# Loading the first projection's weights behind the first token tile, and transposing later token tiles ahead of their own projection, in a five-layer transformer kernel

## Chip, cores and metric

The kernel runs on one core of a Trainium2 chip. The metric is the device time of one launch in microseconds; the time before is the median of three runs. The profile is of a fourth execution, which the hardware profiler recorded.

## What is computed

Five blocks in fp32 on 512 tokens of width 1024: layers of the kinds MLA, SWA, FOX and again MLA, and then a second block of mixers, a gated feed-forward part and a last gate. Only the first steps of the first MLA layer matter here:

```python
h = x @ w_in
cq, ckv, k_rope, gate = h[..., :c1], h[..., c1:c2], h[..., c2:c3], h[..., c3:]
q = (_rmsnorm(cq, q_norm) @ w_q_up).reshape(B, S, MLA_HEADS, MLA_NOPE_DIM + MLA_ROPE_DIM)
kv = (_rmsnorm(ckv, kv_norm) @ w_kv_up).reshape(B, S, MLA_HEADS, MLA_NOPE_DIM + MLA_V_DIM)
```

`cq` has 384 columns, `ckv` 256, `k_rope` 32.

## The kernel before

Tokens are handled in four tiles of 128 (T = 4), the width of 1024 in eight blocks of 128. Each fp32 operand is held as a high part and a low part (`hi`, `lo`), and each product is three matmuls (`mm3`, lines 155 to 159): hi by hi, lo by hi, hi by lo.

**Start.** `__init__` loads the identity. `run` calls `load_x`, which loads the four token tiles (512 KB each) and transposes each on PE with the identity (`to_T`, line 248: two groups of four 128x128 transposes into a PSUM tile `ps_t`, of which there are two; ACT copies the high part, line 184, DVE subtracts for the low part, line 185). Then `mla` loads the tables `cos` and `sin`, and calls `latent` for `ckv` and `k_rope` (288 columns) and again for `cq` (384 columns).

**One latent projection.** `latent` calls `v_proj`. That first asks for eight weight units (`pair_units` for `ckv`): `w` (line 131) loads a unit into a `wr` buffer (there are six), ACT casts it to the high part (L138), POOL or DVE subtracts for the low part (L139). Then, for each token tile, 24 matmuls (8 blocks by 3) fill a PSUM tile `ps_acc` (three buffers), and `evac` normalises that tile: ACT squares and sums (L568), DVE scales the sum (L569), POOL takes the power (L570), DVE multiplies (L571), ACT copies the rope columns (L573), and PE transposes the result (L576 two or three times, L578 once for the rope columns), after which ACT and DVE split it again.

**After the latents** come 24 matmuls of the first gate (512 columns), and then the products on `cq`, the first of which is PE's matmul `ps_acc<-cq,wh` on L157.

**Order.** A scheduler in the build places the instructions of all engines by its own cost estimates, so the order on an engine is not the order of the code. On the chip, each engine takes its instructions in the order placed. SP issues all DMAs; the program gives them eight semaphores in turn (DMAHW0 to DMAHW7), and a DMA waits until the one eight before it has landed, so at most eight are on the way.

Of the kernel before, what the change touches and what calls it, by code (L numbers as in the profile page):

```python
# [15 lines left out]
P, S, D, T = 128, 512, 1024, 4  # L16
# [53 lines left out]

NORM = ("2222", "1122", "0111", "1111")

FOFF = [0, 128, 384, 768]


class Act:


    def __init__(s, hi, lo, n):
        s.hi, s.lo, s.n = hi, lo, n  # L80
# [8 lines left out]
class Kern:  # L89
    def __init__(s, ctx, tc, I, C):  # L90
        s.tc, s.nc, s.I, s.C = tc, tc.nc, I, C
        s.ctx = ctx
        s.sb = ctx.enter_context(tc.tile_pool(name="sb", bufs=1))
        s.dram = ctx.enter_context(tc.tile_pool(name="dram", bufs=1, space=bass.MemoryType.DRAM))
        s.phase_pool, s.phase_tags = None, {}
        s.ps = ctx.enter_context(tc.tile_pool(name="ps", bufs=1, space=PSUM))
        nc = s.nc
        s.ident = s.const("c_ident")
        s.small = s.sb.tile([P, 32], F32, name="small")
        nc.vector.memset(s.small[:, 0:4], -0.5)  # L100
        nc.vector.memset(s.small[:, 4:5], 1e-6)
        nc.vector.memset(s.small[:, 5:6], 1.0)
        s.x = []
        s.rel = None
        s.step = 48

# [159 lines left out]
    def pair_units(s, W, n, c0, cn, dve=False):  # L266

        us = []
        if "hid" in s.phase_tags:
            for k in range(0, n, 2):  # L270
                u = s.t("hid", [P, 4, S], R)
                us += [s.w(W, k + e, 1, c0, cn, u[:, 2 * e:2 * e + 1], u[:, 2 * e + 1:2 * e + 2], dve and e) for e in range(2)]
            return us
        for k in range(n):
            nq = s.phase_tags["qk"]
            if k >= nq + s.phase_tags.get("v", 0):
                us.append(s.w(W, k, 1, c0, cn, "pth", "ptl", dve and k % 2))
            else:
                u = s.t("qk" if k < nq else "v", [P, 2, S], R)
                us.append(s.w(W, k, 1, c0, cn, u[:, :1, :cn], u[:, 1:, :cn], dve and k % 2))  # L280
        return us

    def out_proj(s, W, o, evac, banks=None, oi=5, split_last=False):
# [196 lines left out]
    def mla(s, j, li, xT, g_next):  # L480
        nc, I = s.nc, s.I
        if s.x:
            s.spill_x()
        Win, Wq, Wkv, Wo = I["mla_w_in"][j], I["mla_w_q_up"][j], I["mla_w_kv_up"][j], I["mla_w_out"][j]
        cos = s.t("rope", [P, S], name="cos")
        sin = s.t("rope", [P, S], name="sin")
        nc.sync.dma_start(cos, s.C["c_cos"])
        nc.sync.dma_start(sin, s.C["c_sin"])
        krf = s.t("f", [32, S])
        ckv = s.latent(Win, 384, 288, 256, I["mla_kv_norm"][j], xT, "ckv", krf)  # L490
        cq = s.latent(Win, 0, 384, 384, I["mla_q_norm"][j], xT, "cq")
        kr = s.t("kr", [32, 2, S], R)
        s.rope(krf, cos[:32], sin[:32], kr, 32)
        oT = s.act(8)
        scale = 96.0 ** -0.5
        G = {}

        def queries(g):
            us = [s.w_heads(Wq, k, g * 384, 64, 32) for k in range(3)]
            ps = s.p("acc")  # L500
            for k in range(3):
                h, l = us[k]
                s.mm3(ps, h[:, 256:], l[:, 256:], cq.h(k), cq.l(k), k == 0, k == 2)
            qr = s.t("qr", [P, 2, S], R)
            s.rope(ps, cos, sin, qr, P)
            return us, qr

        def values(g):
            us = [s.w_heads(Wkv, k, g * 512, 64, 64) for k in range(2)]
            vt = [s.t("x", [P, T, 2, 2, 64], R, name="v") for _ in range(2)]  # L510
            for t in range(T):
                ps = s.p("acc")
                c = slice(t * P, (t + 1) * P)
                for k in range(2):
                    h, l = us[k]
                    s.mm3(ps[:, :256], ckv.h(k)[:, c], ckv.l(k)[:, c], h[:, 256:], l[:, 256:], k == 0, k == 1)
                s.v_split(ps[:, :256], [v[:, t] for v in vt])
            return us, vt

        def prep(p):  # L520
            g, pr = divmod(p, 2)
            if ("q", g) not in G:
                G["q", g] = queries(g)
            q_us, qr = G["q", g]
            c = slice(pr * P, (pr + 1) * P)
            ps = s.p("acc")
            for k in range(3):
                h, l = q_us[k]
                s.mm3(ps, h[:, c], l[:, c], cq.h(k), cq.l(k), k == 0, k == 2)
            rr = lambda e: slice(64 * pr + 32 * e, 64 * pr + 32 * e + 32)  # L530
            qt = s.split_heads(ps, lambda e: qr[rr(e)])
            if ("v", g) not in G:
                G["v", g] = values(g)
            kv_us, vt = G["v", g]
            ps = s.p("acc")
            for k in range(2):
                h, l = kv_us[k]
                s.mm3(ps, h[:, c], l[:, c], ckv.h(k), ckv.l(k), k == 0, k == 1)
            kt = s.split_heads(ps, lambda e: kr)
            if pr and g < 3:  # L540
                G["q", g + 1] = queries(g + 1)
            return qt, kt, vt[pr]

        def head(d, p, e):
            qt, kt, v = d
            (qh, ql), (kh, kl) = s.parts(qt[e]), s.parts(kt[e])

            def s_mm(out, i, k0):
                c, kk = slice(i * P, (i + 1) * P), slice(k0 * P, (i + 1) * P)
                return s.mm3(out, qh[:96, c], ql[:96, c], kh[:96, kk], kl[:96, kk], True, True)  # L550

            return s.attend(s_mm, [0] * T, s.causal, scale, s.vsel(v, e))

        s.pairs(range(8), prep, head, Win, 672, xT, oT)
        return s.layer_end(Wo, oT, li, g_next)
# [70 lines left out]
    def v_proj(s, W, c0, n, a, evac, more="p", first=False):  # L626

        kk = 2 if n <= 256 else 1
        if kk == 2:
            us = [s.w(W, k, kk, c0, n) for k in range(0, a.n, kk)]  # L630
        elif more == "p":
            ph, pl = s.t("p", [P, 2, n], R), s.t("p", [P, 2, n], R)
            us = ([s.w(W, k, 1, c0, n, dve=first) for k in range(a.n - 2)]
                  + [s.w(W, a.n - 2 + i, 1, c0, n, ph[:, i:i + 1], pl[:, i:i + 1], first) for i in range(2)])
        else:
            us = s.pair_units(W, a.n, c0, n, first)
        for t in range(T):
            ps = s.p("acc")
            c = slice(t * P, (t + 1) * P)
            for k in range(a.n):  # L640
                h, l = us[k // kk]
                s.mm3(ps[:, :n], a.h(k)[:, c], a.l(k)[:, c], h[:, k % kk], l[:, k % kk], k == 0, k == a.n - 1)
            evac(t, ps)
# [38 lines left out]
    def fox(s, j, li, xT, g_next):  # L682
# [40 lines left out]
        def prep(p):  # L723
# [9 lines left out]
            for e in range(2):  # L733
                cr = s.bcast_row(rows[2 * p + e], "rope")
                b = s.t("qr" if e else "qk", [P, 2, S], name="b").rearrange("p a b -> p (a b)")
                for i in range(3):
                    nc.gpsimd.tensor_add(b[:, FOFF[i]:FOFF[i + 1]], cr[:, :(i + 1) * P], s.causal(i))
                nc.gpsimd.tensor_add(cr[:, 384:], cr[:, 384:], s.causal(0))
                bs.append([b[:, FOFF[i]:FOFF[i + 1]] for i in range(3)] + [cr])
            qt = s.split_q(qps or s.proj(Win, p * P, P, xT))  # L740
# [21 lines left out]
        nc.gpsimd.tensor_sub(lo, a[:n], hi.bitcast(F32))  # L762

    def load_x(s, x, xT):
        for t in range(T):
            xt = s.t("x", [P, D])
            s.nc.sync.dma_start(xt, x[t * P:(t + 1) * P])
            s.to_T(xt, t, xT)
        s.x_src = x
        s.spilled = False  # L770
        s.mask = None
# [365 lines left out]
```

## Time and profile before

| | us |
|---|---|
| runs of before | 1758.92, 1760.01, 1761.11 (median 1760.01) |
| profiled execution, its time | 1762.84 |
| profiled execution, its span | 1761.1 |

The profiled execution's own time is 2.83 us above the median of the runs; its span, first to last instruction, is 1.7 us shorter than that time. Times in the trace count from the span's start. PE was busy for 96% of the span, DVE 55%, ACT 50%, POOL 49%; the mean granted clock of TensorE was 0.979. Idle time of an engine matters only where PE, or the end, waits for it.

### The profile page before, as it was taken

What the parts mean: (1) busy time and instruction counts of PE and PEld (TensorE: products, weight loads), DVE (VectorE), ACT (ScalarE), POOL (GpSimd) and SP (SyncE); (2) the same over time, 40 slices, a digit from 0 to 9 for tenths busy, and PEclk for the clock granted to TensorE, in tenths of its full rate; (3) what the DMA queues carried; (4) which work ended last, traced back from release to release, by engine and by line L of the source; (5) the groups of instructions that cost most, each with busy time, mean ns of one, the idle gap of its engine ahead of it and who ended that gap; (6) DMA issues with size and microseconds to landing.
All of it is one profiled execution on the core that took longest, in us unless ns stands there. A gap on an engine that the chain in (4) does not pass through costs nothing.

```text
span 1761.1 us, 25691 instructions
## 1 busy us (share of the span) xinstructions
PE 1684.8 (96%) x8818; PEld 1435.2 (81%) x8818; DVE 962.0 (55%) x2223; ACT 873.8 (50%) x2054; POOL 854.4 (49%) x775
## 2 busy tenths in 40 slices
PE   8999999999999999999999998999999999999999
PEld 7888878887788888778888877877778888888877
DVE  4587654677654665766587665599544222210053
ACT  4576543666445655633576642755544333332351
POOL 1644534444255665616644523745644444443571
PEclk9999999999999999999999998999999999999999
DMA  5434534322032333314444523332332333332332
GB/s 169 132 98 114 165 104 124 99 70 87 26 97 81 101 88 93 116 51 127 120 110 103 176 61 74 91 81 64 114 90 83 98 96 96 96 100 80 105 99 72
DMA packets 190339, 173.91 MB, mean 99 GB/s; under 512 B 14280, under 2 KB 154952, under 8 KB 190208
## 3 DMA queue, kind: packets, MB, share of 16 engines
q1 hardware_dynamic: 190208, 172.27, 33.9%
q8 instruction: 70, 1.15, 0.3%
q14 instruction: 61, 0.50, 0.1%
HBM read 150.94 MB, written 6.87 MB: 90 GB/s over the span
## 4 chain that ended last, share of the span: by engine, by line
PE 52%; DVE 9%; ACT 2%; issue 2%; POOL 2%; DMA 1%; SPq 0%; ACTq 0%; POOLq 0%; DVEq 0%
PE ps_acc L157 11%; PE ps_acc L158 11%; PE ps_acc L159 11%; PE ps_s L158 4%; PE ps_s L157 4%; PE ps_s L159 4%; PE ps_o L452 2%; PE ps_t L443 2%; DVE p L427 1%; DVE sel L926 1%; ACT p L419 1%; DVE m L925 1%; DVE p L403 1%; PE ps_s L238 1%; DVE ptl L185 1%
## 5 line engine op out<-in xcount | busy, mean ns | idle before, releaser
L139 POOL TENSOR_TENSOR wl<-wr,wh 128x512 fp32r<-128x512 f32 (+2 forms) x362 | 472.7, 1316 | 421.5 <-ACT wh L138 408.7
L138 ACT CAST wh<-wr 128x512 fp32r<-128x512 f32 (+2 forms) x368 | 223.6, 613 | 364.9 <-PE ps_acc L158 125.1
L157 PE MATMUL ps_acc<-act,wh 128*128 128x512 f32 (+1 forms) x880 | 331.5, 377 | 0.9 <-DVE v L620 0.8
L158 PE MATMUL ps_acc<-act,wh 128*128 128x512 f32 (+1 forms) x880 | 330.2, 375 | 0.3 <-DVE act L185 0.2
L159 PE MATMUL ps_acc<-act,wl 128*128 128x512 f32 (+1 forms) x880 | 330.1, 375 | 0.0
L157 PEld LDWEIGHTS ps_acc<-act,wh 128*128 128x128 f32 x880 | 165.6, 188 | 27.9 <-PE ps_acc L159 1.2
L159 PEld LDWEIGHTS ps_acc<-act,wl 128*128 128x128 f32 x880 | 165.3, 188 | 27.5
L158 PEld LDWEIGHTS ps_acc<-act,wh 128*128 128x128 f32 x880 | 165.4, 188 | 27.0 <-DVE act L185 0.7
L419 ACT ACTIVATE p<-p,st 128x256 f32<-128x256 f32 (+3 forms) x288 | 153.5, 537 | 32.8 <-DVE st L410 17.3
L157 PE MATMUL ps_acc<-wh,act 128*128 128x256 f32 (+3 forms) x384 | 134.5, 350 | 7.7 <-ACT act L469 3.1
L185 DVE TENSOR_TENSOR ptl<-ps_t,pth 128x512 fp32r<-128x512 f32 (+1 forms) x200 | 117.6, 597 | 38.5 <-ACT pth L184 37.7
L184 ACT CAST pth<-ps_t 128x512 fp32r<-128x512 f32 (+1 forms) x200 | 100.3, 516 | 72.5 <-PE ps_t L443 63.0
L443 PE MATMUL ps_t<-c_ident,p 128*128 128x128 f32 x672 | 116.9, 283 | 17.3 <-DVE p L427 12.4
L427 DVE TENSOR_SCALAR p<-p,st 128x256 f32<-128x256 f32 (+3 forms) x264 | 132.1, 559 | 1.8
L159 PE MATMUL ps_acc<-wh,act 128*128 128x256 f32 (+3 forms) x384 | 130.7, 341 | 0.1
L158 PE MATMUL ps_acc<-wl,act 128*128 128x256 f32 (+3 forms) x384 | 130.4, 340 | 0.0
L443 PEld LDWEIGHTS ps_t<-c_ident,p 128*128 128x128 f32 x672 | 82.0, 143 | 33.7 <-DVE p L427 13.2
L452 PE MATMUL ps_o<-pth,v 128*128 128x256 f32 (+3 forms) x288 | 90.1, 318 | 6.3 <-DVE og L463 4.4
L452 PE MATMUL ps_o<-ptl,v 128*128 128x256 f32 (+3 forms) x288 | 88.2, 335 | 4.3 <-DVE ptl L185 4.2
L157 PEld LDWEIGHTS ps_acc<-wh,act 128*128 128x128 f32 x384 | 77.8, 203 | 16.0 <-ACT act L469 3.3
L158 PEld LDWEIGHTS ps_acc<-wl,act 128*128 128x128 f32 x384 | 77.7, 202 | 5.1 <-issue 0.5
L159 PEld LDWEIGHTS ps_acc<-wh,act 128*128 128x128 f32 x384 | 77.1, 201 | 5.5 <-DVE act L185 0.3
(371 smaller groups left out, 3801.3 us busy)
## 6 DMA issues: line engine op xcount, KB each, us to landing
wr<-in_w_gate_up_dram SPq DMA_DIRECT2D x88, 256.0 KB, 2.8
wr<-in_fox_w_in_dram SPq DMA_DIRECT2D x60, 256.0 KB, 3.1
wr<-in_w_in_dram SPq DMA_DIRECT2D x48, 256.0 KB, 2.9
wr<-in_w_down_dram SPq DMA_DIRECT2D x44, 256.0 KB, 2.6
wr<-in_swa_w_in_dram SPq DMA_DIRECT2D x40, 256.0 KB, 2.9
wr<-in_mla_w_in_dram SPq DMA_DIRECT2D x32, 256.0 KB, 3.1
qk<-qk SPq DMA_DIRECT2D x32, 256.0 KB, 3.1
wr<-in_mla_w_out_dram SPq DMA_DIRECT2D x32, 256.0 KB, 3.5
```

The costliest lines, as they stand in the source:

```text
L138: nc.scalar.copy(h, raw)
L139: (nc.vector if dve else nc.gpsimd).tensor_sub(l, raw, h.bitcast(F32))
L157: mm(out, lh, rh, start=first, stop=False)
L158: mm(out, lh, rl, start=False, stop=False)
L159: return mm(out, ll, rh, start=False, stop=last)
L184: s.nc.scalar.copy(hi, src)
L185: s.nc.vector.tensor_sub(lo, src, hi.bitcast(F32))
L238: mm(out, q[:, e, c], kd[:, kk], start=True, stop=False)
L419: nc.scalar.activation(a, a, AF.Exp, bias=st[:, 1, i:i + 1], scale=scale, accum_out=st[:, 2, i:i + 1])
L427: nc.vector.tensor_scalar_mul(a, a, st[:, 3, i:i + 1])
L443: nc.tensor.transpose(ps[:, n:n + P], sc[:, c:c + P], s.ident)
L452: nc.tensor.matmul(o[:, j * P:j * P + m], vj, pp[:, c:c + m], start=first, stop=k == 1 and grp[-1] == max(2, grp[-1]) and j == grp[-1], sk ...
```

## The change

`load_x` now issues only the first token tile's load, puts ten identity-by-identity transposes into a `ps_t` tile, and leaves two lists: `late_loads` (loads of tiles 1 to 3) and `late` (the transposes of tiles 0 to 3). `pair_units` issues one of the late loads after each of weight units 6, 7 and 8 (k = 5, 6, 7). `v_proj` runs `late[t]` just ahead of the matmuls of token tile t. `mla` asks for `cos` and `sin` after the first `latent`.

```diff
+WARM = 10
...
-        s.x = []
+        s.x, s.late, s.late_loads = [], [], []
...
                 us.append(s.w(W, k, 1, c0, cn, u[:, :1, :cn], u[:, 1:, :cn], dve and k % 2))
+            if k >= 5 and s.late_loads:
+                s.late_loads.pop(0)()
         return us
...
-        nc.sync.dma_start(cos, s.C["c_cos"])
-        nc.sync.dma_start(sin, s.C["c_sin"])
         krf = s.t("f", [32, S])
         ckv = s.latent(Win, 384, 288, 256, I["mla_kv_norm"][j], xT, "ckv", krf)
+        nc.sync.dma_start(cos, s.C["c_cos"])
+        nc.sync.dma_start(sin, s.C["c_sin"])
...
+        late, s.late = s.late, []
         for t in range(T):
+            if late:
+                late[t]()
             ps = s.p("acc")
...
     def load_x(s, x, xT):
-        for t in range(T):
-            xt = s.t("x", [P, D])
-            s.nc.sync.dma_start(xt, x[t * P:(t + 1) * P])
-            s.to_T(xt, t, xT)
+        nc = s.nc
+        xs = [s.t("x", [P, D]) for _ in range(T)]
+        load = lambda t: nc.sync.dma_start(xs[t], x[t * P:(t + 1) * P])
+        load(0)
+        warm = s.p("t")
+        for k in range(WARM):
+            nc.tensor.transpose(warm[:, k % 4 * P:(k % 4 + 1) * P], s.ident, s.ident)
+        s.late_loads = [lambda t=t: load(t) for t in range(1, T)]
+        s.late = [lambda t=t: s.to_T(xs[t], t, xT) for t in range(T)]
```

Lines of the changed kernel are two to seven higher: line 248 becomes 250, 157 to 159 become 159 to 161, 576 and 578 become 580 and 582, 138 becomes 140, 568 becomes 572.

**PE, around the first normalised tile.** Before, the 24 matmuls of three token tiles (72 in all, mixed) stand ahead of the first transposes of a normalised tile; the last of them and what follows:

```order
L157 MATMUL ps_acc<-pth,act 128x288
L158 MATMUL ps_acc<-ptl,act 128x288
L159 MATMUL ps_acc<-pth,act 128x288
L576 MATMUL ps_t<-c_ident,f 128x128 [waits DVE_49]
L576 MATMUL ps_t<-c_ident,f 128x128
L578 MATMUL ps_t<-c_ident,f 32x128 [waits Activation_49]
L157 MATMUL ps_acc<-qk,act 128x288 [waits PE_49]
```

In the change, the same transposes stand behind the 24 matmuls of token tile 0 alone, and ahead of all work of tile 1:

```order
L160 MATMUL ps_acc<-ptl,act 128x288 [waits DVE_49]
L161 MATMUL ps_acc<-pth,act 128x288
L580 MATMUL ps_t<-c_ident,f 128x128 [waits DVE_49]
L580 MATMUL ps_t<-c_ident,f 128x128
L250 MATMUL ps_t<-c_ident,x 128x128 [waits DMAHW1_49,PE_49]
L250 MATMUL ps_t<-c_ident,x 128x128 x3
L582 MATMUL ps_t<-c_ident,f 32x128 [waits Activation_49]
L159 MATMUL ps_acc<-qk,act 128x288 [waits Activation_49]
L160 MATMUL ps_acc<-qk,act 128x288
L250 MATMUL ps_t<-c_ident,x 128x128 [waits DVE_49]
L250 MATMUL ps_t<-c_ident,x 128x128 x3
L161 MATMUL ps_acc<-qk,act 128x288
```

The waits on PE are, in order: for DVE's multiply of tile 0 (f), for the load of token tile 1 (x), for ACT's high part of tile 1's first four blocks, and for DVE's low part of them. The same piece stands between tiles 1 and 2; between 2 and 3 it differs in that 21 matmuls of `cq` (384 columns) stand between the two matmuls and the second group of transposes.

**SP, the first DMAs.** Before:

```order
L110 DMA c_ident<-in_c_ident_dram 128x128
L767 DMA x<-in_x_dram 128x1024 x4
L487 DMA cos<-in_c_cos_dram 128x512
L488 DMA sin<-in_c_sin_dram 128x512
L256 DMA f<-in_mla_kv_norm_dram 128x256
L135 DMA wr<-in_mla_w_in_dram 128x288 [waits DMAHW0_49]
```

In the change:

```order
L112 DMA c_ident<-in_c_ident_dram 128x128
L775 DMA x<-in_x_dram 128x1024
L258 DMA f<-in_mla_kv_norm_dram 128x256
L137 DMA wr<-in_mla_w_in_dram 128x288 x5
L137 DMA wr<-in_mla_w_in_dram 128x288 [waits DMAHW0_49]
L775 DMA x<-in_x_dram 128x1024 [waits DMAHW1_49]
L775 DMA x<-in_x_dram 128x1024 [waits DMAHW2_49]
L137 DMA wr<-in_mla_w_in_dram 128x288 [waits DMAHW3_49,Pool_49]
L137 DMA wr<-in_mla_w_in_dram 128x288 [waits DMAHW4_49,DVE_49]
L775 DMA x<-in_x_dram 128x1024 [waits DMAHW5_49]
```

Six weight units moved ahead of token tiles 1 and 2; units 7 and 8 stand behind those two tiles, because they wait for a `wr` buffer.

**ACT, between the squares of tile 0 and those of tile 1, in the change:**

```order
L572 ACTIVATE f,st<-ps_acc 128x256 [waits PE_49]
L140 CAST wh<-wr 128x384 [waits DMAHW0_49]
L577 COPY f<-ps_acc 128x32 [waits DVE_49]
L140 CAST wh<-wr 128x384 [waits DMAHW1_49]
L140 CAST wh<-wr 128x384 [waits DMAHW2_49]
L186 CAST act<-ps_t 128x4x128 [waits PE_49]
L583 COPY f<-ps_t 32x128 [waits PE_49]
L186 CAST ckv<-ps_t 128x2x128
L140 CAST wh<-wr 128x384 [waits DMAHW3_49]
L140 CAST wh<-wr 128x384 [waits DMAHW6_49]
L140 CAST wh<-wr 128x384 [waits DMAHW7_49]
L186 CAST act<-ps_t 128x4x128 [waits PE_49]
```

Casts of `cq`'s weights (384 columns) moved between the copies of tile 1: three ahead of its first high part, three more ahead of its second, and another two ahead of its squares.

Past the first layer's `cq` the order is the same on all engines, apart from a few places: around the end of the FOX layer and the start of the second MLA layer, groups of up to five matmuls stand up to 40 places earlier or later on PE, and in the second block's mixers some transposes and copies trade places.

## Rows read from the trace of the kernel before

**Rows 1.** The page, busy time of the engines over the span.

```profile
PE 1684.8 (96%) x8818; PEld 1435.2 (81%) x8818; DVE 962.0 (55%) x2223; ACT 873.8 (50%) x2054; POOL 854.4 (49%) x775
```

**Rows 2.** Waits of PE, 0 to 60 us: total us, times, longest us.

```profile
PE ps_t L248 <- DMA x<-in_x_dram: 4.9, 1, 4.9
PE ps_t L576 <- DVE f L571: 2.1, 2, 2.0
```

**Rows 3.** Timeline of PE, 0 to 60 us: start us, us, what [idle before <-releaser].

```profile
4.87 1.94 PE L248 MATMUL ps_t<-c_ident,x 128*128 128x128 f32 x8 [4.87 <-DMA x<-in_x_dram]
...
12.39 0.66 PE L248 MATMUL ps_t<-c_ident,x 128*128 128x128 f32 x4 [0.68 <-DVE act L185]
12.81 0.64 PE L157 MATMUL ps_acc<-qk,act 128*128 128x288 f32 x3
...
22.69 0.29 PE L159 MATMUL ps_acc<-pth,act 128*128 128x288 f32 x1
24.95 0.58 PE L576 MATMUL ps_t<-c_ident,f 128*128 128x128 f32 x2 [1.97 <-DVE f L571]
...
26.74 0.44 PE L159 MATMUL ps_acc<-qk,act 128*128 128x288 f32 x1
26.98 0.44 PE L157 MATMUL ps_acc<-qk,act 128*128 128x288 f32 x1
...
40.45 0.49 PE L576 MATMUL ps_t<-c_ident,f 128*128 128x128 f32 x3
...
55.68 0.73 PE L157 MATMUL ps_acc<-cq,wh 128*128 128x512 f32 x2 [0.57 <-ACT cq L184]
```

**Rows 4.** Timeline of all engines, 22.5 to 31 us, the normalising of tile 0.

```profile
22.99 0.38 ACT L568 ACTIVATE f<-ps_acc 128x256 f32<-128x256 f32 x1
...
24.41 0.48 DVE L571 SCALAR_TENSOR_TENSOR f<-ps_acc,st,f 128x256 f32<-128x256 f32 x1
```

**Rows 5.** Windows: busy us by engine, PEclk, DMA share, GB/s.

```profile
25.00:26.00 1.00, 1.00 (x5) 0.93 (x6) 0.00 (x0) 0.34 (x3) 0.00 (x0) 0.55 1.05 350
...
29.00:30.00 1.00, 1.00 (x10) 1.00 (x9) 0.00 (x0) 0.00 (x0) 0.00 (x0) 1.00 0.00 0
```

**Rows 6.** Token tiles, 0 to 14 us: duration ns min/median/max, first and last start.

```profile
L248 PE MATMUL ps_t<-c_ident,x x32: 272/421/477, 4.9 to 13.6; 128*128 128x128 f32 x32
```

**Rows 7.** Timelines of ACT and DVE, 5.5 to 7.5 us, splitting one group.

```profile
5.99 0.59 ACT L184 CAST act<-ps_t 128x512 fp32r<-128x512 f32 x1 [3.98 <-PE ps_t L248]
...
6.61 0.69 DVE L185 TENSOR_TENSOR act<-ps_t,act 128x512 fp32r<-128x512 f32 x1 [5.68 <-ACT act L184]
```

**Rows 8.** First weight unit: its DMA issue at 4.67, KB, us to landing.

```profile
wr<-in_mla_w_in_dram SPq DMA_DIRECT2D x1, 144.0 KB, 7.3
```

**Rows 9.** Windows of the start, as in rows 5.

```profile
0.00:5.00 5.00, 0.13 (x1) 0.16 (x2) 0.12 (x3) 1.28 (x1) 0.20 (x4) 1.00 0.60 175
5.00:10.00 5.00, 3.90 (x17) 2.97 (x18) 2.09 (x4) 2.35 (x4) 0.00 (x0) 1.00 0.94 364
10.00:15.00 5.00, 4.32 (x29) 3.92 (x30) 3.99 (x6) 3.83 (x10) 2.23 (x3) 1.00 0.82 267
15.00:20.00 5.00, 5.00 (x40) 5.00 (x39) 3.50 (x7) 2.69 (x6) 1.34 (x2) 1.00 0.91 268
20.00:25.00 5.00, 3.03 (x24) 2.81 (x22) 3.55 (x8) 2.85 (x8) 0.55 (x1) 1.00 0.86 242
```

**Rows 10.** Weight units, 0 to 30 us: casts and subtractions, ns min/median/max.

```profile
L138 ACT CAST qk<-wr x7: 432/435/439, 12.2 to 15.8; 128x288 fp32r<-128x288 f32 x7
L138 ACT CAST wh<-wr x6: 513/514/515, 17.8 to 21.1; 128x384 fp32r<-128x384 f32 x6
L139 DVE TENSOR_TENSOR qk<-wr,qk x3: 466/835/1064, 13.0 to 15.4; 128x288 fp32r<-128x288 f32 x3
```

**Rows 11.** A window with 0.89 us of idle PE in the first layer, as in rows 5.

```profile
220.00:222.00 2.00, 1.11 (x7) 0.55 (x5) 2.00 (x5) 1.98 (x7) 0.13 (x1) 1.00 0.11 34
```

**Rows 12.** Window at the start of the second MLA layer, as in rows 5.

```profile
774.00:784.00 10.00, 6.87 (x26) 5.46 (x26) 2.76 (x4) 2.34 (x4) 1.28 (x1) 0.83 0.11 30
```

More of the change, by code (lines that the diff above doesn't have):

```diff
@@ L486, in mla @@
         sin = s.t("rope", [P, S], name="sin")
+        krf = s.t("f", [32, S])
+        ckv = s.latent(Win, 384, 288, 256, I["mla_kv_norm"][j], xT, "ckv", krf)
         nc.sync.dma_start(cos, s.C["c_cos"])
         nc.sync.dma_start(sin, s.C["c_sin"])
-        krf = s.t("f", [32, S])
-        ckv = s.latent(Win, 384, 288, 256, I["mla_kv_norm"][j], xT, "ckv", krf)
         cq = s.latent(Win, 0, 384, 384, I["mla_q_norm"][j], xT, "cq")
```

## Prediction

> **What bounds the kernel.** I read the busy times first: PE works 96% of the span [rows 1], so a microsecond that PE loses at the start is, as a rule, a microsecond at the end. Then the longest waits of PE over the first 60 us: 4.9 us for the first token tile, 2.0 for one normalised tile [rows 2]. Then PE's timeline for where these lie [rows 3]: transposes from 4.87, the first weight matmul at 12.81, 72 matmuls and four more transposes without a gap to 22.98 (22.69 plus 0.29), idle 1.97, and the first product on cq at 55.68. From that product on both programs have nearly the same order, so I compute when the changed kernel reaches it and carry the difference to the end.
>
> The gap of 1.97 is one chain: ACT squares at 22.99, DVE scales, POOL takes the power, DVE multiplies from 24.41 to 24.89 [rows 4]. Nothing in it can be shortened by the change. It also has an after-effect: at the end of the gap the granted clock falls to half, 1.2 of 2.4 GHz (0.55 in the microsecond after 25, 1.00 again after 29 [rows 5]). Matmuls of 288 columns then start 0.24 apart [rows 3], against 0.13 at full clock (72 of them and four transposes in the 10.2 us from 12.81). From 25.0 to 28.4 that costs about 13 times 0.11 plus 0.2 on three transposes: 1.6 us.
>
> **What the start costs now, and what it cost before.** (1) Tile 0's projection. It ends when weight unit 8 has landed and been split. Before, unit 1 stands in SP's queue behind the identity, four token tiles, cos, sin and the norm row: with itself 64 + 2048 + 512 + 128 + 144 = 2896 KiB, 2.97 MB, and it landed at 4.67 + 7.3 = 11.97 [rows 8]. In the change unit 8 has 64 + 512 + 128 + 864 + 1024 + 288 = 2880 KiB with itself, since units 7 and 8 stand behind token tiles 1 and 2. DMA was nearly full in that stretch before (364 GB/s, share 0.94 [rows 9]), so unit 8 should land at about 11.9. With 0.43 for its cast, about 0.8 for its subtraction [rows 10] and the last matmuls, tile 0 ends at about 13.7. Unit 1, with 848 KiB ahead of and in it, lands at about 6, so most of the 24 matmuls run early; but the last two units hold the end. The ten identity transposes and the eight of tile 0 (about 0.22 apart: eight in 1.94 [rows 3]) run before 6.7, under the weights' loading, and cost nothing; without that cover they would cost 2 us.
>
> (2) All the rest up to the product on cq. Before, 12.81 to 55.68 is 42.9. Taking off tile 0's 24 matmuls (3.1), four token transposes (0.5), the gap (1.97) and the clock (1.6) leaves 35.7. That remains to be done after tile 0.
>
> (3) Token transposes. Before, 28 of 32 ran in the wait for the weights. Now the 24 of tiles 1 to 3 come between matmuls: 24 times 0.11 (three in 0.49, one of 0.27 at its shortest [rows 3, 6]), 2.6 us.
>
> (4) New waits. PE now takes the transposes of normalised tile 0 right after tile 0's matmuls, and all of tile 1 is queued behind them. So the chain of 2.0 us lies open, and again behind tile 1 and tile 2: 6.0. Then come four token transposes, and the next matmul wants ACT's copy of them: 0.59 [rows 7] and a little latency, 0.65, three times: 1.95. Two matmuls later the second group wants DVE's 0.69 [rows 7], less 0.26 of matmuls: 0.45, twice (for tile 3 the 21 cq matmuls cover it): 0.9. Tile 3's own chain is covered only by eight cq matmuls (1.4): 0.65 more. Together 9.5.
>
> (5) Late weights on ACT. Before tile 1's squares ACT must cast all eight cq units. The last ends 5704 KiB into the queue, 5.84 MB; before, that much had moved by about 21.9 (875, 2695, 4030, 5370 KB at 5, 10, 15, 20 us, then 242 per us [rows 9]), and landing lagged by 1.0 (unit 1: 2.97 MB were moved at 11.0). That gives 22.9, with two casts of 0.51 [rows 10] 24: up to 3 us after tile 1's matmuls would end at full clock, 1.3 after they end at half. A faster queue makes it nothing. I take 1.0, bounds 0 and 3.
>
> The moved cos and sin are first used after 49 us and are covered by some 30 us; the norm row of cq now waits for PE's transposes of tile 2, lands some 3 us later, and is wanted only after tile 3: nothing, and what stands behind it on SP waits for POOL anyway.
>
> Sum without the clock: 13.7 + 35.7 + 2.6 + 9.5 + 1.0 = 62.5, against 55.68: 6.8 us later. (6) The clock: each of three gaps is the known one of 1.97 with another 0.65 behind it, so I expect each to bring the same fall: three times 1.6, 4.8 us (the one of before is already taken off). Total 11.6 us. The profiled execution took 1762.84, 2.8 above the median; the sum is a difference, and I set it on the median: 1760.0 + 11.6 = **1771.6 us**, slower.
>
> Does transposing warm the clock? The page reads 1.00 before 25 us, but the token transposes start 0.22 apart up to about 11.5 and 0.13 apart at 12.39 (four in 0.66 [rows 3]), with nothing but transposes run before: half clock, then full. By this the identity transposes may bring the rise some microseconds earlier, which the wait for unit 8 hides. The Trainium skill (TensorE: Matmul & The Clock Gate, Part 4: PE-mode transpose) states that transposes do not bring TensorE to its full rate; the trace disagrees, by the 0.13. By that rule tile 0's last five matmuls would run at half clock, 0.5 us more: 1772.1.
>
> **Rivals.** *The clock stays up.* All waits as above, but no fall, or one: 6.8 to 8.4, with fewer late weights hidden; about **1768**. For it: in another stretch 0.89 us of gaps in 2 us left the clock at 1.00 [rows 11]. Against it: the only gap of this very chain did bring it down [rows 3, 5]. The Trainium skill (TensorE: Matmul & The Clock Gate, Why this matters for your kernels) warns only of longer gaps between bursts than these; by it there would be no fall and the time is this rival's.
>
> *The chains are hidden, and the kernel is faster.* If the normalising of each tile ran beside the next tile's transposes and matmuls, terms (4), (5) and (6) would vanish: 13.7 + 35.7 + 2.6 = 52.0, 3.7 sooner, **1756.3**. It decides itself at the matmul behind the normalised tile: PE comes out ahead only if a tile change costs under 1.2 us of waiting and clock rather than 4.7. For it: the first weight matmul does start some 5 us sooner. Against it: the order puts the waiting transposes ahead of everything of the next tile.
>
> *Given back later.* The scheduler also moved matmuls at the start of the second MLA layer, where PE idles 3.1 of 10 us and the clock is at 0.83 [rows 12], 1.7 lost by it: at most 4.8 could come back (or as much be added). With the first rival's 6.8, that is 2 us later, **1761.5**: no change.
>
> *Worse:* weights at their late bound (2.0 more), tile 0 one microsecond later and a fall that lasts on through a second gap (1.6): about **1776**.
>
> **How the numbers follow.** Forecast 0.50 (its own range 1769 to 1774), clock stays up 0.24, worse 0.09, given back 0.09, faster 0.08. A measurement of this kernel tells about 0.2%, 3.5 us, from no change, so faster is 0.08 (1756.3 is just beyond), same 0.09, slower 0.83. The range from 1764 to 1778 takes in the forecast, the first rival with its unknowns (0 to 3 us of late weights, a few at the second layer's start) and the worse case, and leaves out the last two.
>
> **What would show it.** Right: tile 0's last matmul near 13.7; three gaps of about 2 us on PE ending at DVE's L575; gaps of 0.5 to 0.7 at L159 on ACT's L186; the granted clock at half behind each; the product on cq near 67. The sum is wrong if the last matmul of tile 0 lies beyond 15 (the queue), if the gaps are there but the clock is not (1768), or if the product on cq comes before 56.

## The result and the profile after

| us | before | changed |
|---|---|---|
| median of the runs | 1759.47 (4 runs) | 1774.79 (4 runs) |
| profiled execution, its time | 1762.84 | 1774.51 |
| profiled execution, its span | 1761.1 | 1772.7 |
| mean granted clock in it | 0.979 | 0.977 |
| first product on cq | 55.68 | 68.94 |

The changed kernel is slower: 1.0089 times the time before, interval 1.0072 to 1.0107. Measured again beside the experiments (e8 below) it was 1.0063 [1.0046, 1.0081]. The forecast was 1771.6 us, 11.6 above before; the two spans differ by 11.6, the medians by 15.3, and by 11.9 in e8. One execution of the kernel before, beside e1 to e4, took 2069.75 us in a slow state, and the ratios leave it out.

The page of the changed kernel, busy times, which answers to [rows 1]: PE is busy 5.5 us longer, with ten more instructions, and the rest of the longer span is idle.

```profile
PE 1690.3 (95%) x8828; PEld 1438.8 (81%) x8828; DVE 960.5 (54%) x2223; ACT 873.8 (49%) x2054; POOL 853.4 (48%) x775
```

Waits of PE in the changed kernel, 0 to 60 us (total, times, longest), which answer to [rows 2]. The 4.9 us on the first token tile have become 2.7 for the identity, and the identity transposes fill the rest up to 4.98. The 2.0 on a normalised tile has become 6.3 in four, and a wait on ACT's copies is new.

```profile
PE ps_t L580 <- DVE f L575: 6.3, 4, 2.0
PE ps_acc L159 <- ACT act L186: 2.8, 4, 1.4
PE ps_t L779 <- DMA c_ident<-in_c_ident_dram: 2.7, 1, 2.7
```

The timeline of PE in the same kernel, which answers to [rows 3], shows where they lie.

```profile
2.73 2.40 PE L779 MATMUL ps_t<-c_ident 128*128 128x128 f32 x10 [2.73 <-DMA c_ident<-in_c_ident_dram]
4.98 1.75 PE L250 MATMUL ps_t<-c_ident,x 128*128 128x128 f32 x8
8.11 0.40 PE L159 MATMUL ps_acc<-qk,act 128*128 128x288 f32 x1 [1.38 <-ACT act L186]
...
13.78 0.29 PE L161 MATMUL ps_acc<-pth,act 128*128 128x288 f32 x1
15.98 0.44 PE L580 MATMUL ps_t<-c_ident,f 128*128 128x128 f32 x2 [1.91 <-DVE f L575]
16.26 0.72 PE L250 MATMUL ps_t<-c_ident,x 128*128 128x128 f32 x4
16.77 0.42 PE L582 MATMUL ps_t<-c_ident,f 128*32 128x128 f32 x1
17.65 0.61 PE L159 MATMUL ps_acc<-qk,act 128*128 128x288 f32 x1 [0.46 <-ACT act L186]
...
22.18 0.44 PE L161 MATMUL ps_acc<-qk,act 128*128 128x288 f32 x1
22.42 0.44 PE L159 MATMUL ps_acc<-qk,act 128*128 128x288 f32 x1
...
23.81 0.29 PE L160 MATMUL ps_acc<-ptl,act 128*128 128x288 f32 x1
23.94 0.30 PE L161 MATMUL ps_acc<-pth,act 128*128 128x288 f32 x1
26.14 0.44 PE L580 MATMUL ps_t<-c_ident,f 128*128 128x128 f32 x2 [1.91 <-DVE f L575]
...
36.34 0.44 PE L580 MATMUL ps_t<-c_ident,f 128*128 128x128 f32 x2 [1.97 <-DVE f L575]
...
68.94 0.73 PE L159 MATMUL ps_acc<-cq,wh 128*128 128x512 f32 x2 [0.57 <-ACT cq L186]
```

Read it tile by tile. Tile 0's last matmul starts at 13.78 (forecast: tile 0 ends near 13.7). Then, three times, the same pattern: 1.9 to 2.0 us idle until DVE's L575, the tile's transposes with the next token tile's among them, 0.46 us idle until ACT's copy, then matmuls 0.24 apart (22.18 to 22.42), and 0.13 apart only at the end (23.81 to 23.94). The windows of the same stretch, columns as in [rows 5], give the clock: the granted clock is about two thirds of full from 10 to 40 us, that is, at half for most of it. The first stretch at half clock lies ahead of any chain: tile 0's own matmuls are 0.24 apart from 9.80 to 12.45, and then wait 0.26 us for the last weights.

```profile
5.00:10.00 5.00, 3.22 (x17) 2.76 (x17) 2.40 (x4) 3.11 (x8) 1.97 (x3) 0.98 1.02 359
10.00:15.00 5.00, 3.82 (x18) 3.26 (x16) 1.71 (x4) 1.24 (x4) 1.36 (x3) 0.68 1.03 393
15.00:20.00 5.00, 3.56 (x16) 2.85 (x17) 4.34 (x9) 4.22 (x11) 0.41 (x1) 0.66 0.99 318
20.00:25.00 5.00, 4.23 (x20) 4.00 (x19) 1.84 (x5) 1.42 (x5) 0.00 (x0) 0.66 0.81 232
25.00:30.00 5.00, 3.40 (x16) 2.75 (x17) 1.51 (x3) 1.57 (x5) 0.55 (x1) 0.68 0.02 4
30.00:35.00 5.00, 4.38 (x21) 4.14 (x19) 0.71 (x2) 0.67 (x3) 0.00 (x0) 0.63 0.00 0
35.00:40.00 5.00, 3.20 (x14) 2.81 (x15) 1.65 (x4) 1.19 (x4) 0.55 (x1) 0.71 0.20 35
40.00:45.00 5.00, 5.00 (x33) 4.97 (x32) 0.63 (x1) 0.59 (x1) 0.00 (x0) 0.95 0.03 4
```

The loads cannot explain the later gaps: from 25 us DMA moves next to nothing. PE waits for arithmetic on one tile.

### The profile page after: what moved, and what is told of

It is laid out like the page before. It is cut to its first block, busy times and chain, and to the rows that moved or that the text cites. A ratio compares the mean times of both kernels' runs of the same rounds, so it can differ in the third digit from the quotient of the medians.

```text
span 1772.7 us, 25706 instructions
## 1 busy us (share of the span) xinstructions
PE 1690.3 (95%) x8828; PEld 1438.8 (81%) x8828; DVE 960.5 (54%) x2223; ACT 873.8 (49%) x2054; POOL 853.4 (48%) x775
## 4 chain that ended last, share of the span: by engine, by line
PE 53%; DVE 7%; issue 2%; POOL 2%; ACT 2%; DMA 1%; SPq 0%; POOLq 0%; ACTq 0%; DVEq 0%
PE ps_acc L159 11%; PE ps_acc L160 11%; PE ps_acc L161 11%; PE ps_s L160 4%; PE ps_s L159 4%; PE ps_s L161 4%; PE ps_o L456 2%; PE ps_t L447 2%; DVE p L431 1%; ACT p L423 1%; DVE p L407 1%; DVE sel L939 1%; DVE m L938 1%; PE ps_s L240 1%; PE ps_s L241 1%
```

## The experiments

Theory: the transposes placed just ahead of each tile's matmuls leave the normalising open (PE has no other work while it runs), and the idle time brings the clock down. Rivals: the new order of the loads is the loss; the waits alone count; the identity transposes matter. Each run is read at two places: where the first product on cq starts, in its one profiled execution, and its time against before's on the same chip. Run to run, one kernel's times spread by some 12 us (before: 1754.6 to 1766.7 in the first set), so the first place tells more about the start than the second.

| run | edit, from the changed kernel | cq | time | ratio to before [95%] |
|---|---|---|---|---|
| e1 | transposes to fill the gaps | 63.96 | 1773.12 | 1.0060 [1.0042, 1.0078] |
| e2 | normalising one tile later | 55.92 | 1765.04 | 1.0016 [0.9999, 1.0033] |
| e3 | loads in the old order | 74.33 | 1782.75 | 1.0115 [1.0097, 1.0134] |
| e4 | no identity transposes | 68.60 | 1775.01 | 1.0076 [1.0051, 1.0100] |
| e5 | e2, token transposes one tile ahead | 52.67 | 1757.66 | 0.9971 [0.9957, 0.9986] |
| e6 | all token transposes ahead | 51.65 | 1761.73 | 1.0000 [0.9985, 1.0015] |
| e7 | kernel before, normalising later | 54.37 | 1760.46 | 0.9988 [0.9974, 1.0002] |
| e8 | none | 70.61 | 1773.93 | 1.0063 [1.0046, 1.0081] |
| e9 | e6 and e2 together | 51.69 | 1759.91 | 0.9994 [0.9982, 1.0006] |
| e10 | e5 without identity transposes | 53.52 | 1758.39 | 0.9992 [0.9978, 1.0006] |
| e11 | e5 again | 53.94 | 1758.88 | 0.9987 [0.9967, 1.0007] |

The medians of before in the four sets were 1761.34 (e1 to e4), 1762.03 (e5 to e8), 1759.51 (e9, e10) and 1760.66 (e11).

**e1: waits and clock apart.** In the first latent's evacuation, behind the squares of tiles 0 to 2:

```diff
             nc.scalar.activation(c[:, :m], ps[:, :m], AF.Square, accum_out=st[:, 0:1])
+            if rest is not None and t < T - 1 and not s.spilled:
+                fill = s.p("o")
+                for k in range(11):
+                    nc.tensor.transpose(fill[:1, k % 4 * P:(k % 4 + 1) * P], st[:, 0:1], s.ident)
```

> The changed kernel, with eleven transposes of the identity's kind (one column of squares as the tile) added behind each of the first three normalised tiles, so that PE works while it waits for the chain; nothing waits for them and every wait stays. They need the squares' sum, so they can start about 0.6 us into a gap of 1.9. Theory (waits, and half a clock behind them): the three gaps on the normalised tile shrink on PE's timeline but the tile's transposes start at the same distance from the tile's last matmul, and the clock stays at 2.4 GHz; the stretches at half speed took about 7.5 us of the changed kernel, so the product on cq comes at 61.5 (60 to 63.5) instead of 68.94 and the time falls by 5 to 9 us to about 1767. Rival 1 (the waits alone count, the clock is a passenger): the product on cq stays within 1.5 us of 68.94. Rival 2 (these transposes do not hold the clock): the granted clock reads 0.5 as before in most of 16 to 40 us and nothing moves.

Timeline of PE in e1. The first gap is split in two, but the tile's transposes still start 2.2 us behind its last matmul (14.36 to 16.56), as in the changed kernel (13.78 to 15.98).

```profile
14.36 0.30 PE L161 MATMUL ps_acc<-pth,act 128*128 128x288 f32 x1
15.22 1.36 PE L576 MATMUL ps_o<-c_ident,st 128*1 128x128 f32 x11 [0.56 <-ACT f L572]
16.56 0.44 PE L584 MATMUL ps_t<-c_ident,f 128*128 128x128 f32 x2
...
18.12 0.40 PE L159 MATMUL ps_acc<-qk,act 128*128 128x288 f32 x1 [0.56 <-ACT act L186]
...
22.47 0.29 PE L161 MATMUL ps_acc<-pth,act 128*128 128x288 f32 x1
...
63.96 0.73 PE L159 MATMUL ps_acc<-cq,wh 128*128 128x512 f32 x2 [0.57 <-ACT cq L186]
```

Windows of e1, columns as in [rows 5]:

```profile
15.00:20.00 5.00, 4.01 (x29) 3.00 (x30) 3.60 (x9) 3.70 (x12) 0.55 (x1) 1.00 0.86 298
20.00:25.00 5.00, 4.34 (x33) 3.37 (x32) 3.16 (x8) 2.09 (x7) 0.55 (x1) 1.00 0.84 232
```

Tile 0's squares on ACT, in the changed kernel and then in e1:

```profile
14.12 0.38 ACT L572 ACTIVATE f<-ps_acc 128x256 f32<-128x256 f32 x1 [1.56 <-PE ps_acc L161]
14.70 0.38 ACT L572 ACTIVATE f<-ps_acc 128x256 f32<-128x256 f32 x1 [1.11 <-PE ps_acc L161]
```

The clock stays full, and matmuls run 0.13 apart. From the squares of tile 0 (14.70 here, 14.12 in the changed kernel) to the product on cq it is now 49.3 us instead of 54.8: the half clock took **5.6 us** (5.9 against e8, 15.47 to 70.61), and the waits with all that goes with them the rest of the loss. That refutes both rivals. The product on cq came just behind the expected 60 to 63.5, since tile 0 ended 0.6 later and the expectation took every microsecond at half clock as half lost, 7.5 in all. That the clock stays up is not seen in one execution alone: the mean granted clock was 0.978 to 0.984 in e1's twelve runs, and 0.975 to 0.980 in the ten of the changed kernel. The Trainium skill (TensorE: Matmul & The Clock Gate, Part 4: PE-mode transpose) states that transposes do not count as busy for the clock in the way that matmuls do. Here they were all that filled the three gaps, and no fall came: this trace disagrees. The expected fall of the time, by 5 to 9 us, is not shown: by the ratios to before it is 5.1 us against the first measurement of the changed kernel and 0.5 against the second. That is taken up below.

**e2: the chain covered.** One tile's evacuation is held back behind the next tile's matmuls:

```diff
+        held = []
         for t in range(T):
...
-            evac(t, ps)
+            if late:
+                held.append((t, ps))
+                if t:
+                    evac(*held.pop(0))
+            else:
+                evac(t, ps)
+        for h in held:
+            evac(*h)
```

> The changed kernel, with the normalising of a token tile issued behind the next tile's matmuls instead of straight behind its own. Theory (the three open chains and the half clock they bring are the loss): tile 0's chain lies under tile 1's matmuls; of the three gaps of 1.9 us at most one is left, the clock stays up for most of 16 to 40 us, and the product on cq comes at 54 to 58 instead of 68.94; the time is 1758 to 1764, about that of the kernel before, perhaps below it. Rival (the new order of the loads, weight units behind token tiles, is the loss): the gaps go, but PE waits for weights or token tiles in their place, and the product on cq stays above 64, the time above 1769.

Timeline of PE in e2. One gap is left instead of three; tile 1's matmuls were done by then too, since the scheduler mixed them into tile 0's wait for the last weight units.

```profile
16.33 0.29 PE L161 MATMUL ps_acc<-pth,act 128*128 128x288 f32 x1
18.79 0.44 PE L580 MATMUL ps_t<-c_ident,f 128*128 128x128 f32 x2 [2.17 <-DVE f L575]
...
24.40 0.38 PE L580 MATMUL ps_t<-c_ident,f 128*128 128x128 f32 x2
```

The product on cq is 13 us earlier, with the new loads untouched. The theory holds; the rival on the loads falls. The time, 1765.04, lies 1 us above the expected 1758 to 1764.

**e3: the loads alone.** All token tiles, cos and sin are loaded ahead of the weights again; the transposes stay ahead of each projection.

```diff
...
-        s.late_loads = [lambda t=t: load(t) for t in range(1, T)]
+        for t in range(1, T):
+            load(t)
```

> The changed kernel with the loads in the old order (four token tiles, cos and sin, then the weights); the transposes of tiles 1 to 3 stay just ahead of their own projection. Theory (open chains and clock): tile 0 ends when the eighth weight unit lands behind 3904 KiB, at about 16 instead of 14.1, and everything behind it is as in the changed kernel: gaps of 1.9 three times, half clock behind each, product on cq at 70 to 71.5, time 1775 to 1778. Rival (the order of the loads is the loss): the product on cq comes back by several us, to 62 or below, and the time to 1768 or below.

Worse, as the theory had it, and by more than expected: PE waits 5.4 us for the first weight unit, comes out of that at half clock, and tile 0's squares start at 18.85 instead of 14.12 (15.47 in e8). So the new order of the loads gains some 3 to 5 us at tile 0.

```profile
12.28 0.61 PE L159 MATMUL ps_acc<-qk,act 128*128 128x288 f32 x1 [5.44 <-ACT qk L140]
13.15 0.61 PE L160 MATMUL ps_acc<-qk,act 128*128 128x288 f32 x1 [0.27 <-POOL qk L141]
20.80 0.44 PE L580 MATMUL ps_t<-c_ident,f 128*128 128x128 f32 x2 [2.21 <-DVE f L575]
```

**e4: the identity transposes** (`WARM = 0` and the loop taken out).

> The changed kernel without its ten identity transposes. Theory: they run under the load of the first weights and cost nothing; without them tile 0's first matmuls may run at half clock, which the wait for the last weight units hides; tile 0 ends at 14.1 and the product on cq comes at 68.9, each within 0.5; the time is within 3 us. Rival (the rise of the clock that they bring is worth something): product on cq 0.5 to 1.5 us later. Rival 2 (they delay the first token tile's transposes): 0.5 us or more sooner.

The product on cq came where it was expected, but by two misses that cancel. Timeline of PE in e4: matmuls are still 0.24 apart at 23 us, where those of the changed kernel were 0.14 apart for a moment before 10 us (9.26, 9.40, 9.54) and 0.13 apart at the end of tile 0 (13.39 to 13.78). Tile 0's squares start at 16.10, later by 0.6 (than in e8) to 2.0.

```profile
23.07 0.44 PE L160 MATMUL ps_acc<-qk,act 128*128 128x288 f32 x1
23.32 0.44 PE L161 MATMUL ps_acc<-qk,act 128*128 128x288 f32 x1
...
25.38 0.29 PE L160 MATMUL ps_acc<-ptl,act 128*128 128x288 f32 x1
25.52 0.29 PE L161 MATMUL ps_acc<-pth,act 128*128 128x288 f32 x1
27.71 0.44 PE L580 MATMUL ps_t<-c_ident,f 128*128 128x128 f32 x2 [1.90 <-DVE f L575]
```

Behind the gap that ends at 27.71 the clock did not fall; behind the next, of 1.97, it did (0.72 in the microsecond from 37, 0.50 in the next two). The same gap can cost its clock or not. This rests on one execution here; the gap of 2.11 us in e7 below is a second one without a fall.

**e5: the next tile's transposes ahead as well.** From e2:

```diff
-            if late:
-                late[t]()
+            if late and t == 0:
+                late[0]()
...
+            if late and t < T - 1:
+                late[t + 1]()
             if late:
                 held.append((t, ps))
```

> The changed kernel with the normalising of a tile behind the next tile's matmuls, as in the run before with that edit, and each tile's token transposes issued one tile ahead as well. There, one gap of 2.2 us and a copy's 0.57 were left at tile 0, with half clock to 23.7 behind them, and the product on cq came at 55.92. Theory (open chains and half clock are the loss): the order now puts the transposes of tile 2 and fourteen matmuls ahead of tile 0's normalised transposes, so that gap goes, and the clock stays up: product on cq at 51.5 to 53, 2.7 to 4.2 us ahead of the kernel before; if the rest of the program takes the same time as in the earlier run (about 3 us more than before's), the time is within 2 us of before's, otherwise 3 to 4 below it. Rival (the start is bound by the landing of weights and token tiles): the gap is replaced by waits on loads, product on cq at 55 or later, time 2 us or more above before's.

Waits of PE in e5, 0 to 60 us: nothing of the chain is left but 0.2, and the clock is full from 13 us.

```profile
PE ps_acc L159 <- ACT act L186: 2.2, 2, 1.3
PE ps_acc L159 <- ACT cq L186: 0.6, 1, 0.6
...
PE ps_t L580 <- DVE f L575: 0.2, 1, 0.2
```

The start is 3.0 us ahead of before's, and the time 4.4 below it, the one edit whose interval lies below 1. Run again:

> The quickest kernel so far once more (normalising behind the next tile's matmuls, token transposes one tile ahead), since it was the best of five that start 1.3 to 4 us ahead of the kernel before and the other four were within 2 us of it. If the start is what makes it quicker: product on cq at 52 to 54, time 1.5 to 4.5 us below before's, ratio 0.9975 to 0.9991. If its first ratio of 0.9971 was chance: a ratio of 0.999 to 1.001.

It came out 1.8 below before, with an interval that holds 1. Both runs fit a gain of about 3 us; by the second alone it is not shown.

**e6: all transposes ahead, new loads.**

```diff
+        for f in late:
+            f()
         for t in range(T):
-            if late:
-                late[t]()
```

> The changed kernel with the transposes of all four token tiles issued ahead of the projection, as in the kernel before; loads in the new order, identity transposes kept. Theory: the order of the loads by itself costs nothing, and what costs is the transposes just ahead of each tile's matmuls, which leave the normalising open. PE then mixes the later tiles' transposes into the wait for the last weight units, and has at most one open chain; product on cq at 52 to 56, time 1757 to 1765. Rival (the order of the loads is a loss of its own, the last token tile landing late): PE waits for token tiles 2 and 3 by more than 3 us, product on cq at 59 or later, time 1766 or above.

This splits the change in two at the product on cq: new loads with the old place of the transposes gain 4.0 us (55.68 to 51.65), and moving the transposes into the tiles then loses 17.3 (51.65 to 68.94). No wait of 0.2 us or more is left on PE from 9 us to 50.

```profile
51.65 0.73 PE L159 MATMUL ps_acc<-cq,wh 128*128 128x512 f32 x2 [0.57 <-ACT cq L186]
```

The time does not show the 4.0 us: its ratio is 1.0000.

**e7: the kernel before, with e2's edit** (in the first latent of both MLA layers).

> The kernel before, with the normalising of a token tile of the first latent (and of the second MLA layer's) issued behind the next tile's matmuls. Theory: the one gap of 1.97 and the 1.6 us of half clock behind it go, and with them up to 3.6 us: product on cq at 52 to 54 instead of 55.68, time 2 to 4 us below before's. Rival (a gap of another kind takes its place, as when the copies for the first product on cq come later by as much): product on cq at 55 to 57, time within 2 us of before's.

The gap stayed: 2.11 us, ending at 25.18. Only the fall behind it did not come (matmuls 0.13 apart from 25.7), and the product on cq is 1.3 us earlier; the time does not tell it from before. Why the edit could not cover the gap is seen on ACT in the kernel before itself, here from 19 to 24 us:

```profile
20.13 1.49 ACT L138 CAST wh<-wr 128x384 fp32r<-128x384 f32 x3 [0.33 <-DMA wr<-in_mla_w_in_dram]
22.57 0.51 ACT L138 CAST p<-wr 128x384 fp32r<-128x384 f32 x1 [0.95 <-DMA wr<-in_mla_w_in_dram]
22.99 0.38 ACT L568 ACTIVATE f<-ps_acc 128x256 f32<-128x256 f32 x1
```

and on PE, tile 0's last matmul:

```profile
18.21 0.30 PE L159 MATMUL ps_acc<-pth,act 128*128 128x288 f32 x1
```

Tile 0 had been done since 18.5. Its squares stood on ACT behind the casts of cq's weights, the last of which waited 0.95 for its DMA, and came at 22.99 (23.23 in e7) by that, when PE had done all three tiles that it could. So the gap of before was the same chain of 2 us, but what started it was a queue, not the order of PE. That is read from the trace; no run took those casts away.

**e8: the changed kernel again.**

> The changed kernel itself, beside the others on their chip, as their measure. Expected: 13 to 16 us above before's median, product on cq at 68.9 where the clock falls behind all three gaps, and up to 5.6 us earlier in an execution where it falls behind fewer, since without the identity transposes the same gaps brought it down only once.

All three gaps came again, and three stretches at half clock, the first from 14.5 already, ahead of its gap. Tile 0's squares started at 15.47, 1.35 later, since PE waited 1.17 and 0.47 us for the last two units. The time was 11.9 above before's median, a little less than expected.

**e9 and e10: what is left.**

> The changed kernel with all token transposes ahead of the projection, as in the earlier run with that edit (product on cq at 51.65), and the normalising of a tile behind the next tile's matmuls besides. Theory: with the transposes ahead, no chain was left open there, so there is nothing more for the deferral to cover: product on cq at 51 to 52.5, time within 3 us of that run's. Rival (the normalising still cost something there, under the copies): product on cq a microsecond or more sooner, and the time 2 us or more below before's.

As the theory had it at the product on cq (51.69). The second:

> The quickest kernel so far (normalising behind the next tile's matmuls, token transposes one tile ahead; product on cq at 52.67, 0.9971 of before's time) without the ten identity transposes. In the changed kernel, taking them out left PE at half clock up to 23.7 us and ended tile 0 at 16.1 instead of 14.1 to 15.4. Theory (they bring the clock up earlier, and here PE has work to use it on while the weight units land): half clock up to some 11 us or longer, product on cq 1 to 4 us later, at 53.7 to 56.7, time 1 to 4 us more. Rival (the landing of the weight units hides it): product on cq within 0.7 us of 52.67, time within 2 us.

Neither clearly: 53.52 lies between e5's 52.67 and e11's 53.94, which are one kernel. That the identity transposes are worth anything is not shown.

## Why the prediction was right

**Sign, size and place** were right, though the gap of before, from which the price of a chain was taken, had another cause than the three of the changed kernel (e7). In the changed kernel the squares of tiles 0 to 2 do wait for PE (14.12, 24.27 and 34.48). The theory, that the chain of each tile lies open because the order puts the waiting transposes ahead of all of the next tile, is what e2, e5 and e6 undo. That the spans differ by just the 11.6 of the forecast is luck: the terms were off by up to 2.5 us, and their errors and those of the rest of the program cancel. Term by term, to the product on cq, forecast at 67.3 (62.5 and 4.8) and found at 68.94:

- *(1) Tile 0 at 13.7:* its last matmul started at 13.78 and its squares at 14.12; in e8 the squares at 15.47. The reckoning by the queue held in the first of these: the casts of units 7 and 8 start at 11.79 and 12.12, in e8 at 12.79 and 13.16.
- *(4) New waits, 9.5:* e1 has them at full clock: 1.9 to 2.0 for each of three chains (1.92, 1.92 and 1.99), three copies at 0.56, two subtractions at 0.2, and 0.55 at tile 3. That is 8.5.
- *(5) Late weights on ACT, 1.0:* nothing. The last two casts start at 20.02, one right after the other, and tile 1's squares wait for PE until 24.27, as this timeline of ACT in the changed kernel shows; in e1, at full clock, they wait for PE too.

```profile
20.02 0.93 ACT L140 CAST p<-wr 128x384 fp32r<-128x384 f32 x2
24.27 0.38 ACT L572 ACTIVATE f<-ps_acc 128x256 f32<-128x256 f32 x1 [3.33 <-PE ps_acc L161]
```

- *(2) and (3), 38.3:* in e1 49.3 less 8.5 is 40.8, 2.5 more. Part of it can be seen: tile 1's matmuls run there from 18.12 to 22.47, 4.35 us, where 24 at 0.13 and four transposes at 0.11 make 3.6. Behind a transpose or a wait, the second matmul starts 0.22 to 0.24 after the first (18.12 to 18.36, 19.25 to 19.47) instead of 0.13, and there are pauses shorter than the timeline lists. I had counted whole instructions and no restarts.
- *(6) The clock, 4.8:* 5.6 by e1. The term was set by the one fall of before (1.6 each); here the stretches behind the first two gaps lasted nearly a whole tile, 6 to 7 us.

So 0.4 too little in (1), 1.0 too much in (4), 1.0 too much in (5), 2.5 too little in (2) and (3), 0.8 too little in (6): 1.7 us too little at the product on cq. The span's difference came out exact because other parts of the program gave 1.7 back. This table has the profiled executions in six parts. The marks between them are the first product on cq, the first on tile z in the FOX layer, the first DMA that writes x out to memory (spilling), the last product on ckv in the second MLA layer, and the last on bd in the second block's mixers.

| us | to cq | cq to FOX's z | z to spilling x | to the last product on ckv | to the last on bd | to the end |
|---|---|---|---|---|---|---|
| before | 55.7 | 467.7 | 275.4 | 180.9 | 248.8 | 532.6 |
| changed | 68.9 | 466.8 | 274.2 | 183.8 | 246.4 | 532.6 |
| changed, e8 | 70.6 | 469.5 | 274.6 | 183.7 | 243.1 | 532.6 |
| e1 | 64.0 | 469.9 | 275.2 | 181.1 | 247.2 | 534.3 |
| e5 | 52.7 | 471.6 | 274.6 | 184.5 | 243.0 | 532.7 |
| e11 (as e5) | 53.9 | 469.1 | 275.9 | 182.0 | 246.6 | 532.8 |

One kernel's own two executions differ by up to 3.6 us in a column. That is as much as any later gain or loss here, so *given back later* is not shown: the stretch with the second MLA layer's start, where I had put it, took 2.9 us longer in the changed kernel, and the next one less. It also blurs e1's gain: against the changed kernel's first execution e1 lost 3.1 us again between cq and z, against its second only 0.4, and 1.7 at the end against both. In *given back later* the sum itself has a slip: 6.8 less 4.8 on 1760.0 is 1762.0, not 1761.5.

**The other rivals.** *The clock stays up* (1768) did not happen by itself; e1 made it happen. Beside the rows: the Trainium skill (TensorE: Matmul & The Clock Gate, Why this matters for your kernels) warns only of longer idle gaps between matmul bursts. Here gaps of 1.9 to 2.0, with another 0.5 behind them, were followed by half clock in five of six cases in the two executions of the changed kernel (the sixth ran at half before), so the traces disagree. Taken from matmul to matmul, with the transposes as idle time, these stretches are 3.5 to 3.6 us (the first 14.07 to 17.65); but that of the kernel before is 2.4 (22.98 to 25.39) and had its fall too, and those of e1 are 3.5 (14.66 to 18.12) and had none. *The chains are hidden* was the right price for another program: it put tile 0's and the later work at a product on cq of 52.0, and e5, which hides them, reaches it at 52.67 (53.94 in e11).

## What to carry to other kernels

When a change lets work start earlier by splitting a batch, look in the order for what each piece ends with: a short chain on other engines that one long batch hides is paid once per piece, and here most often with the clock's fall behind it. Issue a piece's tail behind the next piece's main work, and check in the trace that the tail's first instruction really starts under it: in e2 both pieces ended together, and in e7 it stood behind late weights in its engine's queue. Judge such an edit at the nearest later instruction that all versions share, because 3 us at the start are lost in the scatter of the whole time.

## What was not expected of the hardware

- The clock's row is silent at the start: in e4 the windows from 15 to 25 us read 1.00 while matmuls of 288 columns start 0.24 apart until 23.55 and 0.13 apart from 23.80. The spacing has to be read beside it.
- The same program's mean granted clock differs from execution to execution, and the time with it: in the first set before ran from 1754.59 us at 0.985 to 1766.72 at 0.979. One execution does not fit: beside e11, before read 0.932 and took 1760.88.
- With ten identity transposes ahead, matmuls first ran 0.13 apart by about 9 us in four executions (the changed kernel, e2, e5, e6), between 11 and 13 in three (e1, e8, e9), at 14.5 in e11 and at 18 in e3, behind its wait of 5.4; without them at about 13 us in e10 and at 23.8 in e4. In three of the first four (not in e2) they were 0.24 apart again before 10 us, and until 12.5 to 13.4.
